# A two-block network on one core: the recurrences' instructions handed to the scheduler 400 places further to the front

## Chip, cores and metric

The kernel runs on one core of a Trainium2 chip. The metric is device time in microseconds (us) of one execution. The engines are called as the profile calls them: PE (TensorE, matrix multiplication), PEld (its weight loads), DVE (VectorE), ACT (ScalarE), POOL (GpSimd), SP (SyncE, which issues the DMAs).

## What is computed

The reference is two transformer-like blocks of width 1024 on 256 tokens, in float32. The first block has two attentions, a cross-attention to 256 memory tokens and a gated feed-forward net with a convolution. The second block has two layers over the 256 tokens and 256 context tokens. Each layer mixes by neighbourhood attention, by a convolution and by a recurrence in both directions (RWKV-7, four heads of 64); then comes a dense feed-forward net (layer 0) or one of eight experts with two chosen for each token (layer 1). The recurrence is what the change is about:

```python
def _rwkv7_scan(r, w, k, v, z, b):       # (T, G, H, dh): 512 steps, 2 directions, 4 heads, 64
    def step(S, inp):
        r_t, w_t, k_t, v_t, z_t, b_t = inp
        s_z = jnp.einsum('ghvk,ghk->ghv', S, z_t)
        S = S * w_t[:, :, None, :] + s_z[..., None] * b_t[:, :, None, :] + v_t[..., None] * k_t[:, :, None, :]
        return S, jnp.einsum('ghvk,ghk->ghv', S, r_t)
    _, y = lax.scan(step, jnp.zeros((G, H, dh, dh), jnp.float32), (r, w, k, v, z, b))
    return y
```

The context is scanned first and its last state is the first state of the tokens' scan, so there are four scans of 256 steps in a row: layer 0 context, layer 0 tokens, layer 1 context (only its state is wanted), layer 1 tokens.

## The kernel before

**Streams.** The work is written as Python generators that emit instructions and yield how much they emitted. `par` lets several generators emit in turn, by weights. So the order of emission mixes, for example, a feed-forward net and a recurrence. Behind that, the scheduler of the kernel language makes each engine's list from what was emitted: it takes instructions by their place in the emission as far as what they need allows, and each engine then works through its list strictly in that order. No order is written by hand.

**Stages.** `program` opens and closes buffer pools by stage. Four stages hold a recurrence:

- C0 (426 to about 770 us): `first_ffn` of the first block, the recurrence over the context of layer 0 and its output projection, behind them the context's dense net.
- C1 (about 1003 to 1254 us): that dense net, the recurrence over the tokens of layer 0, behind them the tokens' dense net.
- C2 (1316 to about 1566 us): the rest of the tokens' dense net and the recurrence over the context of layer 1.
- C3 (1566 to about 1854 us): the projections, neighbourhood attention and convolution of layer 1 and the recurrence over the tokens (`mixers`).

Before C0 stands the first block's attention, between C0 and C1 and between C1 and C2 projections and layer 0's attention, and from 1854 us on the experts.

**Full matmuls.** Projections and nets split each fp32 weight slab into a high part `whi` (ACT, L306) and the rest `wlo` (DVE, L307) and add three fp32r matmuls for each product (`mm3`). They write the PSUM tiles `acc` and `accA`, use the whole array (128*128 in the rows below), and have 256 columns.

**Partial matmuls.** The recurrence is cut into four chunks of 64 steps for each pair of heads; `rwkv_unit` makes one unit for each direction (`dr`) and pair (`i`), and PSUM tile `c0` belongs to direction 0, `c1` to direction 1 (the rows below say `c` for both). A unit inverts a triangular 64x64 matrix by doubling, five rounds that depend on each other, each round one batch of matmuls, a DVE or ACT copy out of PSUM, another batch, another copy:

```python
four = [(a, r, h) for a in range(2) for r, h in ((0, 0), (1, 1), (0, 1), (1, 0))]
...
for a, r, h in four:
    self.mm(pp[half[h], r, P + a * 64:P + a * 64 + 64], X[half[r], h, a, :], i64[half[r]])
if j < 6:
    T1 = tl()
    nc.vector.tensor_tensor(out=T1, in0=two(pp, 0), in1=lm2(j), op=ALU.mult)
Y = tl()
self.copy(Y, two(pp, P))
...
for a, r, h in four:
    self.mm(pp[half[r], h, a * 64:a * 64 + 64], Y[half[h], r, a, :], T1[half[h], r, a, :])
```

These matmuls are fp32 and use a quarter of the array (64*64); `four` lets neighbours use quarters with different rows and columns. Other parts of the recurrence use halves (128*64, 64*128). `rwkv_scan` carries the state from chunk to chunk (`Sb`, `go`) with such matmuls into PSUM tile `sm`. A fp32 matmul leaves two records in the trace: eight matmuls are a row with x16.

Of the kernel before, what the change touches and what calls it, by code (L numbers as in the profile page):

```python
# [148 lines left out]
def par(*gens, behind=None):  # L149


    live = []
    for i, g in enumerate(list(gens) + ([behind] if behind else [])):
        g, w, t = (g + (0.0,))[:3]
        live.append([t / w, i, g, w, None, 0.0])
    spent = 0.0
    while any(e[1] < len(gens) for e in live):
        ready = [e for e in live if (e[4] is None or e[4]()) and e[5] <= spent]
        if not ready:
            late = [e for e in live if e[4] is None or e[4]()]  # L160
            if late:
                t = min(e[5] for e in late)
                yield Lat(t - spent)
                spent = t
            else:
                waits = [e[4] for e in live]
                yield lambda: any(w() for w in waits)
            continue
        e = min(ready, key=lambda e: (e[0], e[1]))
        e[4] = None  # L170
        try:
            c = next(e[2])
        except StopIteration:
            live.remove(e)
            continue
        if callable(c):
            e[4] = c
            continue
        cost = c.cost if isinstance(c, Lat) else c or 1.0
        e[0] += cost / e[3]  # L180
        spent += cost
        if isinstance(c, Lat):
            e[5] = spent + c
        if cost:
            yield cost
# [52 lines left out]
class K:  # L238
# [735 lines left out]
                self.mm(ps[:, c:c + 2], sq[:, i, t * P:(t + 1) * P], self.const("hm"))  # L974
        return ps

    def rwkv(self, l, s, u, S0, need_out, st):

        nc = self.nc
        k_, v_ = u[1], u[2]
        st.update(S={}, units=([], []), begun=[0, 0], done=[0, 0], kd={}, y={})

        sq = self.t("d2", [P, 2, T])
        for i in range(2):
            nc.scalar.activation(sq[:, i, :], k_[:, i, :], AF.Square, scale=self.v(f"k_k{l}", i))
        ps = self.head_sums(sq, "c0")
        nv = self.t("sc", [P, 16])[:, :8]
        nc.vector.tensor_scalar(out=nv, in0=ps[:, 0:8], scalar1=1.0, scalar2=1e-12, op0=ALU.mult, op1=ALU.add)  # L990
        kb = self.head_bc(self.rsqrt(nv, 8), "c0")
        kk = self.t("kk", [P, 2, T])
        for i in range(2):
            nc.vector.scalar_tensor_tensor(out=kk[:, i, :], in0=k_[:, i, :], scalar=self.v(f"k_k{l}", i),
                                           in1=kb[:, i, :], op0=ALU.mult, op1=ALU.mult)

        vt = self.t("vt", [P, 2, T])
        pv = self.ps("c1")
        for t in range(2):
            for i in range(2):  # L1000
                nc.tensor.transpose(pv[:, (2 * t + i) * P:(2 * t + i + 1) * P], v_[:, i, t * P:(t + 1) * P],
                                    self.ident)
        self.copy(vt.rearrange("p a b -> p (a b)"), pv)
        yield 2.0
        yield from par(*[(self.rwkv_maps(l, dr, u, kk, vt, need_out, st), 45) for dr in range(2)],
                       *[(self.rwkv_scan(l, s, dr, u, S0, need_out, st), 12) for dr in range(2)])
        if need_out:
            y = st["y"]
            nc.vector.tensor_tensor(out=y[0], in0=y[0], in1=y[1], op=ALU.add)
            st["o"] = y[0]  # L1010
# [367 lines left out]
    def mixers(self, l, x, kv, u, ao, hp, cv, rwkv):  # L1378

        q, k, v = self.t("qkv", [P, 4, T]), self.t("qkv", [P, 4, T]), self.t("qkv", [P, 2, 512])  # L1380
        pr = self.project(l, 0, x, q, k, v, u, hp, "accA", early=True)
        yield from self.until(pr, "ready")

        def rest():
            yield from self.until(pr, "conv")
            yield from par((na(), 100), (self.conformer(l, hp, cv), 20))

        def na():
            yield from pr
            yield from self.na_attn(l, q, k, v, *kv, ao, "accA", "opM")  # L1390
        yield from par((rest(), 130), (rwkv, 93.5))
# [457 lines left out]
```

## Time and profile before

| | |
|---|---|
| median of 3 runs | 2905.23 us (2900.95 to 2911.19) |
| the profiled execution | 2904.22 us, its span 2902.0 us |
| PE busy | 2721.5 us, 94% of the span |
| DVE busy | 2130.2 us, 73% |
| ACT busy | 1703.9 us, 59% |
| DMA | 619.81 MB, 214 GB/s on average |

The span is what the trace covers; the execution takes 2.2 us more. Busy time is the time in which an engine works on at least one instruction. The rows of the trace give start, duration and form of each instruction. Two starts of PE that follow each other say more than a duration, since matmuls are pipelined and overlap.

### The profile page before, as it was taken

The numbers are of one execution on the slowest core, as the hardware profiler recorded it, in microseconds if no ns is written. First come the engines' busy times: TensorE is split into PE (matmuls) and PEld (weight loads), VectorE is DVE, ScalarE is ACT, GpSimd is POOL, SyncE is SP. The second block draws the span as 40 slices with busy tenths as digits, with TensorE's granted clock in tenths as the row PEclk, the third lists the DMA queues.
The fourth block names the chain that finished last, engine by engine and source line by source line (L and its number), as shares of the span: only waits on it lengthen the run. The fifth ranks groups of instructions, "written<-read, shape, count | busy, mean of one in ns | idle before, by whom it ended". The sixth has DMA issues, their size and how long they took to land.

```text
span 2902.0 us, 55553 instructions
## 1 busy us (share of the span) xinstructions
PE 2721.5 (94%) x22026; PEld 2340.4 (81%) x22026; DVE 2130.2 (73%) x3912; ACT 1703.9 (59%) x2709; POOL 79.8 (3%) x229
## 2 busy tenths in 40 slices
PE   7899989999799899999998878799999999999998
PEld 5788888999787688999997866688888878887886
DVE  4458657777668466777566864689888889989897
ACT  4455555554454355455444553478777777777775
POOL 0000000100000000000000010000000000000000
PEclk9899998999899999999999987799999999999998
DMA  7666432345466723444443221479899999999994
GB/s 269 230 196 196 154 101 89 125 125 153 147 215 223 236 85 100 146 147 152 140 139 107 92 59 29 201 282 364 342 347 359 350 350 354 358 338 356 365 353 168
DMA packets 144022, 619.81 MB, mean 214 GB/s; under 512 B 31044, under 2 KB 38536, under 8 KB 100744
## 3 DMA queue, kind: packets, MB, share of 16 engines
q1 hardware_dynamic: 143752, 616.17, 61.0%
q8 instruction: 175, 2.87, 0.4%
q14 instruction: 95, 0.78, 0.1%
HBM read 615.04 MB, written 1.07 MB: 212 GB/s over the span
## 4 chain that ended last, share of the span: by engine, by line
PE 75%; DVE 8%; ACT 4%; issue 2%; DMA 2%; POOL 0%; SPq 0%; ACTq 0%; POOLq 0%; DVEq 0%
PE acc L291 42%; PE py L291 10%; PE accA L291 8%; PE sm L291 6%; PE c L291 6%; DVE wlo L307 1%; DVE wlo L440 1%; PE md L291 1%; PE sm L1571 1%; ACT whi L306 1%; PE accA L505 0%; DMA raw<-mod_w 0%; ACT whi L439 0%; DVE x L939 0%; DVE t L380 0%
## 5 line engine op out<-in xcount | busy, mean ns | idle before, releaser
L440 DVE TENSOR_TENSOR wlo<-raw,whi 128x1024 fp32r<-128x1024 f32 x666 | 779.4, 1220 | 79.8 <-ACT whi L439 73.0
L306 ACT ACTIVATE whi<-raw 128x512 fp32r<-128x512 f32 x764 | 474.3, 629 | 502.1 <-PE acc L291 259.7
L307 DVE TENSOR_TENSOR wlo<-raw,whi 128x512 fp32r<-128x512 f32 x764 | 521.3, 689 | 330.2 <-ACT whi L306 316.8
L439 ACT ACTIVATE whi<-raw 128x1024 fp32r<-128x1024 f32 x666 | 676.7, 1058 | 105.6 <-PE py L291 60.8
L291 PE MATMUL acc<-whi,op 128*128 128x512 f32 (+1 forms) x2048 | 620.8, 379 | 0.0
L291 PE MATMUL acc<-op,whi 128*128 128x256 f32 x2880 | 561.4, 294 | 8.7 <-ACT op L385 3.6
L291 PEld LDWEIGHTS acc<-op,whi 128*128 128x128 f32 x2880 | 460.1, 196 | 36.3 <-issue 13.8
L291 PEld LDWEIGHTS acc<-whi,op 128*128 128x128 f32 x2048 | 378.6, 189 | 71.5 <-issue 3.0
L291 PE MATMUL acc<-op,wlo 128*128 128x256 f32 x1440 | 414.7, 288 | 10.3 <-DVE wlo L307 10.3
L291 PE MATMUL acc<-wlo,op 128*128 128x512 f32 (+1 forms) x1024 | 393.0, 384 | 2.5 <-DVE wlo L440 1.4
L291 PEld LDWEIGHTS acc<-op,wlo 128*128 128x128 f32 x1440 | 281.5, 196 | 13.1 <-DVE wlo L307 12.7
L291 PE MATMUL py<-whi,ht 128*128 128x512 f32 x896 | 291.2, 396 | 0.5 <-ACT ht L306 0.5
L291 PE MATMUL accA<-opM,whi 128*128 128x256 f32 x1408 | 272.0, 292 | 7.7 <-ACT opM L306 3.5
L291 PEld LDWEIGHTS accA<-opM,whi 128*128 128x128 f32 x1408 | 225.0, 196 | 23.7 <-issue 7.7
L291 PEld LDWEIGHTS acc<-wlo,op 128*128 128x128 f32 x1024 | 193.2, 189 | 53.6 <-DVE wlo L440 17.6
L291 PE MATMUL acc<-fh,whi 128*128 128x256 f32 x1056 | 206.1, 293 | 3.0 <-ACT fh L306 1.9
L291 PE MATMUL accA<-opM,wlo 128*128 128x256 f32 x704 | 202.4, 288 | 1.5 <-DVE wlo L307 1.3
L291 PEld LDWEIGHTS py<-whi,ht 128*128 128x128 f32 x896 | 168.7, 188 | 39.3 <-ACT ht L306 0.9
L291 PE MATMUL py<-wlo,ht 128*128 128x512 f32 x448 | 180.6, 403 | 0.3
L291 PEld LDWEIGHTS acc<-fh,whi 128*128 128x128 f32 x1056 | 165.4, 192 | 18.4 <-issue 9.6
L291 PE MATMUL acc<-fh,wlo 128*128 128x256 f32 x528 | 150.4, 285 | 1.9 <-DVE wlo L307 1.9
L291 PEld LDWEIGHTS accA<-opM,wlo 128*128 128x128 f32 x704 | 137.3, 195 | 4.5 <-issue 2.2
(338 smaller groups left out, 3337.2 us busy)
## 6 DMA issues: line engine op xcount, KB each, us to landing
raw<-moe_up SPq DMA_DIRECT2D x112, 1024.0 KB, 7.0
raw<-moe_gate SPq DMA_DIRECT2D x111, 1024.0 KB, 6.8
raw<-moe_down SPq DMA_DIRECT2D x110, 1024.0 KB, 6.8
raw<-w_in SPq DMA_DIRECT2D x120, 512.0 KB, 3.7
raw<-mod_w SPq DMA_DIRECT2D x96, 512.0 KB, 4.5
raw<-ffn_gate SPq DMA_DIRECT2D x44, 512.0 KB, 3.6
raw<-ffn_up SPq DMA_DIRECT2D x44, 512.0 KB, 3.6
raw<-ffn_down SPq DMA_DIRECT2D x40, 512.0 KB, 3.7
```

The lines of the kernel that those rows point to most:

```text
L291: return self.nc.tensor.matmul(out, lhsT, rhs, start=start, stop=stop, **k)
L306: self.nc.scalar.activation(hi, src, AF.Copy)
L307: self.nc.vector.tensor_tensor(out=lo, in0=src, in1=hi.bitcast(F32), op=ALU.subtract)
L439: self.nc.scalar.activation(hi, raw[:, k:k + g, :], AF.Copy)
L440: eng.tensor_tensor(out=lo, in0=raw[:, k:k + g, :], in1=hi.bitcast(F32), op=ALU.subtract)
L1571: nc.tensor.transpose(pt[:, c * P:(c + 1) * P], h[:, c * P:(c + 1) * P], self.ident)
```

## The change

`rwkv` becomes a wrapper. Its former body is now called `recurrence`, and each of its steps is emitted inside `tc.high_priority(400)`: the scheduler treats every instruction of the four recurrences as if it had been emitted 400 places earlier. What is emitted, its order of emission, the buffers and the arithmetic stay; the output projections behind two of the recurrences (`mix_out`) aren't inside.

```diff
-    def rwkv(self, l, s, u, S0, need_out, st):
+    def rwkv(self, *a):
+
+        gen = self.recurrence(*a)
+        while True:
+            with self.tc.high_priority(400):
+                try:
+                    c = next(gen)
+                except StopIteration:
+                    return
+            yield c
+
+    def recurrence(self, l, s, u, S0, need_out, st):
```

What the scheduler makes of it shows in the engines' lists. Names end in the tile's number; `acc`, `whi`, `wlo`, `op` and `fh` belong to a net, `c`, `zt`, `cst`, `t`, `go`, `Sb` and `vt` to a recurrence; the last figure is the size written.

The first place is on PE in C2, one round of one unit. Before:

```order
L291 MATMUL acc_17395<-op_15121,whi_17373 128x256
L291 MATMUL acc_17395<-op_15120,wlo_17374 128x256
L291 MATMUL c_3058_17408<-t_3045_17332,zt_16553 64x64 x8
L291 MATMUL c_3058_17408<-cst_72,t_3045_17332 64x64 x8
L291 MATMUL c_3061_17429<-t_3047_17351,t_3048_17353 64x64 x8
L291 MATMUL acc_17395<-op_15120,whi_17391 128x256
L291 MATMUL acc_17395<-op_15121,whi_17391 128x256
```

The same round with the change:

```order
L291 MATMUL c_3058_17408<-t_3045_17332,zt_16553 64x64
L291 MATMUL c_3061_17429<-t_3047_17351,t_3048_17353 64x64
L291 MATMUL c_3058_17408<-cst_72,t_3045_17332 64x64
L291 MATMUL acc_16595<-op_15120,whi_16626 128x256
L291 MATMUL c_3058_17408<-cst_72,t_3045_17332 64x64
L291 MATMUL acc_16595<-op_15121,whi_16626 128x256
L291 MATMUL c_3058_17408<-cst_72,t_3045_17332 64x64
L291 MATMUL acc_16595<-op_15120,wlo_16627 128x256
L291 MATMUL c_3058_17408<-cst_72,t_3045_17332 64x64
L291 MATMUL acc_16595<-op_15120,whi_16626 128x256
```

The batch of eight into `c_3058_17408` stood in one piece behind `acc_17395`; now it stands beside the earlier `acc_16595`, and single matmuls of the two alternate.

The second place is on PE in C0, a step of the scan (`sm_6487`) and the first batch of a unit (`c_1189_6475`). Before:

```order
L291 MATMUL acc_6423<-op_4846,wlo_6420 128x256
L291 MATMUL c_1189_6475<-cst_72,zt_6361 64x64 x8
L291 MATMUL sm_6487<-go_5971,Sb_6176 64x64 x6
L291 MATMUL acc_6423<-op_4846,whi_6457 128x256
L291 MATMUL acc_6423<-op_4847,whi_6457 128x256
```

With the change:

```order
L291 MATMUL sm_6487<-go_5971,Sb_6176 64x64
L291 MATMUL c_1189_6475<-cst_72,zt_6361 64x64
L291 MATMUL acc_5655<-op_4846,wlo_5603 128x256
L291 MATMUL sm_6487<-go_5971,Sb_6176 64x64
L291 MATMUL c_1189_6475<-cst_72,zt_6361 64x64
L291 MATMUL acc_5655<-op_4846,whi_5602 128x256
L291 MATMUL sm_6487<-go_5971,Sb_6176 64x64
L291 MATMUL c_1189_6475<-cst_72,zt_6361 64x64
```

Here too batches have come apart into a rotation of three streams, one full matmul in each turn.

The third place is on PE in C1, both directions' units: `c_2387_13477` is copied to `t_2388_13486` by DVE, which the batch into `c_2395_13526` reads. Before:

```order
L291 MATMUL c_2387_13477<-t_2380_13441,t_2381_13443 64x64 x8
L291 MATMUL c_2389_13488<-t_2383_13454,zt_12975 64x64 x8
L291 MATMUL c_2389_13488<-cst_72,t_2383_13454 64x64 x8
L291 MATMUL acc_13513<-fh_13112,whi_13458 128x256
...
L291 MATMUL acc_13513<-fh_13112,wlo_13459 128x256
L291 MATMUL c_2395_13526<-t_2388_13486,zt_13025 64x64 x8
```

With the change:

```order
L291 MATMUL c_2389_13488<-t_2383_13454,zt_12975 64x64
L291 MATMUL c_2387_13477<-t_2380_13441,t_2381_13443 64x64
L291 MATMUL c_2389_13488<-t_2383_13454,zt_12975 64x64
L291 MATMUL c_2389_13488<-cst_72,t_2383_13454 64x64 x8
L291 MATMUL c_2395_13526<-t_2388_13486,zt_13025 64x64 x8
L291 MATMUL c_2395_13526<-cst_72,t_2388_13486 64x64 x6
```

Twelve full matmuls stood between the batches of this round and the next; now none does, and the two directions' first batches alternate.

## Rows read from the trace of the kernel before

**Rows 1.** The page: PE's busy share, then PE and its clock in 40 slices.

```profile
PE 2721.5 (94%) x22026; PEld 2340.4 (81%) x22026; DVE 2130.2 (73%) x3912; ACT 1703.9 (59%) x2709; POOL 79.8 (3%) x229
...
PE   7899989999799899999998878799999999999998
...
PEclk9899998999899999999999987799999999999998
```

**Rows 2.** Windows: the four stages, then the recurrences' dense stretches in C0 and C2.

```profile
core 0: us, PE busy (x) PEld busy (x) DVE busy (x) ACT busy (x) POOL busy (x), PEclk, DMA share, GB/s
426.00:771.00 345.00, 321.35 (x3610) 298.76 (x3610) 250.46 (x583) 181.71 (x329) 18.62 (x50) 0.94 0.41 126
1003.00:1254.00 251.00, 235.38 (x2987) 218.57 (x2988) 178.30 (x430) 130.74 (x238) 13.71 (x45) 0.96 0.35 112
1316.00:1566.00 250.00, 238.72 (x3045) 224.99 (x3043) 164.41 (x350) 121.74 (x213) 12.88 (x49) 0.99 0.41 130
1566.00:1854.00 288.00, 241.28 (x2768) 204.47 (x2768) 188.07 (x537) 135.63 (x291) 23.24 (x53) 0.86 0.27 79
452.50:677.00 224.50, 220.80 (x2915) 206.61 (x2913) 167.16 (x387) 121.16 (x226) 11.40 (x30) 0.99 0.39 119
1316.00:1545.00 229.00, 226.41 (x2813) 214.72 (x2815) 153.93 (x311) 114.55 (x197) 11.60 (x43) 1.00 0.43 139
```

**Rows 3.** Longest wait of PE in C0, 452.5 to 677 us: total, times, longest.

```profile
PE acc L291 <- ACT whi L306: 1.8, 3, 0.7
```

**Rows 4.** Timeline of PE in C0: batches and full matmuls. Start, duration, what.

```profile
486.72 0.41 PE L291 MATMUL c<-t,zt 64*64 64x64 f32 x16
486.96 0.41 PE L291 MATMUL c<-cst,t 64*64 64x64 f32 x16
487.30 0.50 PE L291 MATMUL acc<-fh,whi 128*128 128x256 f32 x2
487.64 0.28 PE L291 MATMUL acc<-fh,wlo 128*128 128x256 f32 x1
487.76 0.40 PE L291 MATMUL acc<-fh,whi 128*128 128x256 f32 x2
...
488.71 0.28 PE L291 MATMUL acc<-fh,wlo 128*128 128x256 f32 x1
488.92 0.29 PE L291 MATMUL c<-t,t 64*64 64x64 f32 x4
```

**Rows 5.** Timeline of PE in C2 where single full matmuls stand between quarters.

```profile
1534.08 0.34 PE L291 MATMUL c<-t,t 64*64 64x64 f32 x6
1534.35 0.38 PE L291 MATMUL acc<-fh,whi 128*128 128x256 f32 x1
1534.66 0.34 PE L291 MATMUL c<-t,t 64*64 64x64 f32 x6
1534.93 0.39 PE L291 MATMUL acc<-fh,whi 128*128 128x256 f32 x1
```

**Rows 6.** Waits of PE in C3, 1600 to 1808 us.

```profile
PE c L291 <- ACT t L301: 4.7, 6, 2.4
PE c L291 <- DVE t L1260: 3.4, 5, 1.3
```

**Rows 7.** Windows: a part of C3, the end of C2, C3's second half.

```profile
1740.00:1770.00 30.00, 25.86 (x482) 17.72 (x476) 12.91 (x45) 10.91 (x32) 2.18 (x2) 0.72 0.10 19
1520.00:1564.00 44.00, 33.96 (x645) 30.69 (x646) 25.45 (x70) 16.87 (x33) 1.29 (x6) 0.96 0.25 76
1690.00:1808.00 118.00, 94.24 (x1135) 68.29 (x1132) 61.08 (x222) 51.17 (x135) 18.71 (x34) 0.77 0.14 25
```

**Rows 8.** Timeline of PE in the first of these windows.

```profile
1760.26 0.65 PE L291 MATMUL c<-t,zt 64*64 64x64 f32 x16
1760.69 0.65 PE L291 MATMUL c<-cst,t 64*64 64x64 f32 x16
```

## The prediction

> **What bounds the kernel now.** I began with the page: PE is busy 94% of the span and in most slices 90% or more at the full clock, DVE 73%, ACT 59% [rows 1]. As a busy share is an average, I cut the span at the stages with a recurrence [rows 2]. In C0 PE is busy 321.35 of 345 us, in C1 235.38 of 251, in C2 238.72 of 250, in C3 241.28 of 288; DVE comes second everywhere. Inside the dense stretches, where recurrence and net run together, almost nothing is left: 220.80 of 224.50 us in C0, 226.41 of 229.00 in C2, the clock at 0.99 and 1.00. The view of waits says the same of C0: PE's largest group of waits is 1.8 us in three times [rows 3]. So in C0 and C2 PE works through its list without a stop, and the recurrence's dependent chain, which has many short steps, is hidden behind full matmuls. An order that finishes this chain sooner has nothing to win there. Whatever it makes PE's own list cost, in starts from one matmul to the next, is paid in full, since PE has 2.6 to 3.7 us of slack in each of these stretches.
>
> Idle time of PE that another order could remove lies at the end of C2 (44.00 less 33.96, 10.0 us) and in the second half of C3 (118.00 less 94.24, 23.8 us) [rows 7].
>
> **What a matmul costs in its neighbourhood.** The timeline gives starts. A batch of eight quarter matmuls in a row takes 0.24 us (486.72 to 486.96), a full matmul among its like 0.12 us (487.64 to 487.76) [rows 4]. Going from one kind to the other costs extra. The last batch before a full matmul takes 0.34 us instead of 0.24 (486.96 to 487.30). The first two full matmuls take 0.34 instead of 0.24 (487.30 to 487.64). From the last full matmul to the next quarter it is 0.21 instead of 0.12 (488.71 to 488.92) [rows 4]. That is 0.10 + 0.10 + 0.09 = 0.29 us for leaving the full matmuls' form and coming back, a round trip, apart from a slower start of the quarters, which these rows don't separate.
>
> Single full matmuls between quarters occur a few times before. Their turn, one full matmul and three or four quarters, takes 0.58 us (1534.08 to 1534.66 and 1534.35 to 1534.93) [rows 5]. The work in it is 0.12 for the full one and at most 0.12 for four quarters, half a batch. The remaining 0.34 us is the price of a round trip, with the start of the quarters in it.
>
> The Trainium skill, TensorEngine Tiling (Array Packing), section Tiling Modes, has a rule that speaks against this change: changing the tiling mode, and not merely the tile, drains TensorE. It names no price; the rows above agree with it. By that rule changes between partial forms count too; they grow by about 40, which at half a round trip (0.17) would make the sum 7 us larger.
>
> **The change, part by part.** Nothing is added or removed on any engine; DMAs keep their order but for a few places, and the buffers are the same. What changes is the order of the lists, and I counted on PE's list, stage by stage, how many stretches of full matmuls it has. Every stretch is one round trip.
>
> - C0: 55 stretches before, 244 after, of which 197 hold one full matmul (1 before). The number of matmuls is the same, 1333 full and 761 partial ones. The second place shown in the section on the change is typical.
> - C1: 43 before, 43 after.
> - C2: 46 before, 348 after, 296 with one full matmul (2 before). The first place is typical.
> - C3: 51 before, 63 after.
>
> The extra round trips are 189 + 0 + 302 + 12 = 503. At 0.34 us: C0 64.3, C2 102.7, C3 4.1, together **171 us**. I take 0.34 and not 0.29 since the turns in rows 5 are the ones that the new list is made of. No row shows a turn with a single quarter matmul, and 180 (C0) and 244 (C2) of the new partial stretches hold just one. Below, the price is 0.19: entering (0.09) and the slow first full matmul (0.10) with nothing for leaving. Above, it is 0.68, twice 0.34, if PE is at half its clock (rival 1). Over 503 trips these are 96 and 342 us. No cover hides any of it: PE is the engine that is waited for, and ACT and DVE only get more time.
>
> The second part is new waits. In C1 (third place) twelve full matmuls, 1.44 us, stood between the batches of a round and the batch that reads DVE's copy of them; now one batch of eight does, 0.24 us. I took for each copy the work on PE between the last matmul that it reads and the first that reads it, by the durations above. Under 0.6 us it is in 8 places of C1 (0 before), 4 of C0 (0), 0 of C2 (5) and 11 of C3 (9); between 0.6 and 1.2 us in 15 (2), 12 (0), 6 (1) and 14 (11). What such a place costs C3 shows already: 11 waits of `c` for L301 and L1260 took 8.1 us, 0.74 each [rows 6]. I price the first kind at 0.7 us and the second at 0.3. C0: 2.8 + 3.6 = 6.4. C1: 5.6 + 3.9 = 9.5. C2: -3.5 + 1.5 = -2.0. C3: 1.4 + 0.9 = 2.3. Together **16 us**, with bounds of 0 (the scheduler's guess of readiness holds) and 32 (each twice as long, behind a slab's split on DVE).
>
> The third part is the tail of C2. Before, no full matmul stands behind the recurrence's last `c` matmul in that stage; after, 243 do. The recurrence then no longer drags behind, and up to 10.0 us of idle time [rows 7] could go. But C3 begins with the norm of the net's result, and its chain of small steps, which the recurrence covered in part, would then stand alone. I count 0, with bounds of -10 and +5.
>
> Against the profiled execution (2904.22 us, 1 us under the median of the runs, 2905.23): 2904.2 + 171 + 16 + 0 = 3091; I say **3090 us**, 6.4% longer.
>
> **Rivals.**
>
> 1. *The clock falls where the forms alternate.* Between 1740 and 1770 us PE is busy 25.86 of 30 us with small matmuls, and the granted clock is 0.72 [rows 7]; a batch of eight there takes 0.43 us instead of 0.24 [rows 8], the lower of the two levels. There PE also waits between its batches, and the few turns of rows 5 were run at the full clock. If a third of the 503 round trips fell to 1.2 GHz, each would cost 0.34 us more, 57 us, and the work in them some 0.24 us more each, 40 us: 3090 + 97 = 3187 us.
>
> 2. *A single change of form is cheap.* One quarter matmul between full ones might cost less than the two ends of a longer stretch. For it speaks that no row shows a turn with one quarter; against it, that the turns with three or four cost as much as the long stretches' two ends together. At 0.10 us the 503 trips cost 50, and the time is 2904 + 50 + 16 = 2970 us.
>
> 3. *The other sign: the recurrences leave the end of their stages.* If the idle 10.0 us at the end of C2 and 23.8 us in C3 [rows 7] vanish because the chain starts earlier, 33.8 us are won. This decides only when a round trip costs less than (33.8 - 16) / 503 = 0.035 us, a tenth of what rows 4 and 5 show; with trips free it gives 2904 - 34 + 16 = 2886 us. Against it also speaks that C3's list changes least: 36 full matmuls stood behind the last `c` matmul there, and 35 do now.
>
> 4. *The change does little.* In C1 and C3 the number of round trips hardly moves. Were C0 and C2 like that, the waits alone would be left, 16 us less 10 at the tail: 2910 us. The lists shown exclude it for the order, so it needs free round trips too.
>
> **How the numbers follow.** The forecast has 0.75, rival 1 0.12, rival 2 0.07, rival 3 0.03, rival 4 0.03. The range of the forecast itself goes from 2904 + 96 + 16 - 10 = 3006 us (price 0.19) to 3091 plus the second 16 us of waits, 5 at C2's tail and half of rival 1's 97, 3160 us. I give 3010 to 3170, which leaves out most of rival 1 and rivals 2 to 4. About 0.3% (9 us) is what a measurement of this kernel can tell from no change. Faster than that is rival 3, 0.03; within it falls rival 4, 0.03; slower is everything else, 0.94.
>
> **What would show it.** In the profile after, C0's dense stretch should be about 65 to 70 us longer with PE still busy over 95% of it, C2's about 100 us, C1 some 10 us with new waits of `c` for L1260 and L301 (by their lines after the change, 11 further down), C3 within 10 us, and the experts from the same start to end as before. The number and the durations of the matmuls should be the same, only their starts further apart: a turn of one full and one or two quarter matmuls should take 0.4 to 0.6 us. PE's granted clock in C0 and C2 tells rival 1 from the forecast; a turn under 0.3 us shows rival 2. The prediction is wrong if the long stretches of C0 and C2 don't grow, or if they grow through PE's waits and not through its starts.

## The result and the profile after

The changed kernel takes 3283.91 us (median of 4 runs, 3276.36 to 3311.96) beside 2908.21 us for the kernel before (4 runs on the same chip, 2900.95 to 2911.5). The ratio is 1.1322, with a 95% interval of 1.1289 to 1.1355: 376 us longer, about twice the 186 us that were forecast. The profiled execution (3311.96 us, span 3310.2 us) is the longest of the four; its span is 408 us longer than that of before.

The page of the changed kernel, PE's busy share, then PE and its granted clock in 40 slices, answers to [rows 1]:

```profile
PE 3128.0 (94%) x22026; PEld 2584.6 (78%) x22026; DVE 2137.4 (65%) x3912; ACT 1703.8 (51%) x2709; POOL 78.3 (2%) x229
...
PE   7999989999989999999999989778999999999998
...
PEclk9999977679989999996795599778999999999998
```

The count of PE's instructions is the same, its busy share is the same, and its busy time is 407 us longer. So nearly everything that was lost lies inside PE's busy time. The clock row has two new hollows, at slices 6 to 9 (C0) and 19 to 23 (C2). The windows of the four stages, each from the same place on PE's list to the same place as in the kernel before, and the experts, answer to [rows 2, 7]. C1, C2 and C3 between these places before (C0 stands in [rows 2]):

```profile
1050.00:1191.80 141.80, 135.47 (x2012) 124.19 (x2011) 96.80 (x243) 70.00 (x133) 9.80 (x26) 0.98 0.32 100
1328.00:1558.00 230.00, 224.41 (x2930) 211.98 (x2929) 151.50 (x308) 113.47 (x199) 11.76 (x44) 1.00 0.41 130
1583.00:1808.00 225.00, 193.80 (x2454) 159.73 (x2452) 149.45 (x432) 109.00 (x243) 23.24 (x53) 0.86 0.24 65
```

All four with the change, and the experts:

```profile
core 0: us, PE busy (x) PEld busy (x) DVE busy (x) ACT busy (x) POOL busy (x), PEclk, DMA share, GB/s
454.50:830.00 375.50, 369.87 (x2914) 296.96 (x2912) 169.35 (x386) 122.67 (x228) 10.11 (x30) 0.79 0.22 71
1200.20:1348.00 147.80, 141.83 (x2011) 127.15 (x2011) 97.29 (x243) 68.40 (x132) 9.83 (x26) 1.00 0.30 96
1483.90:1940.50 456.60, 451.92 (x2934) 348.50 (x2934) 151.02 (x305) 112.81 (x196) 9.36 (x40) 0.72 0.21 66
1968.00:2221.00 253.00, 213.17 (x2456) 170.47 (x2455) 156.15 (x444) 108.03 (x243) 23.02 (x53) 0.84 0.20 57
2396.00:3300.00 904.00, 897.67 (x4064) 724.15 (x4062) 796.21 (x791) 678.58 (x766) 0.00 (x0) 1.00 0.91 340
```

| stretch | before, us | after, us | difference | granted clock, before and after |
|---|---|---|---|---|
| C0, dense part | 224.5 | 375.5 | +151.0 | 0.99, 0.79 |
| C1, dense part | 141.8 | 147.8 | +6.0 | 0.98, 1.00 |
| C2, without its tail | 230.0 | 456.6 | +226.6 | 1.00, 0.72 |
| C3, to the recurrence's end | 225.0 | 253.0 | +28.0 | 0.86, 0.84 |

The experts take about as long as before, 904.0 us beside 902.8. PE's idle time in C0 went from 3.7 us to 5.6 (375.50 less 369.87) and in C2 from 5.6 (230.0 less 224.41) to 4.7: the two long stretches grew in PE's starts and not in its waits. C1 grew within PE's busy time too: its idle time was 6.3 us before and is 6.0.

The timeline of PE in C0 shows how, at two places 4 us apart (start, duration, what):

```profile
590.26 0.33 PE L291 MATMUL c<-bcst,t 128*64 128x64 f32 x2
590.52 0.39 PE L291 MATMUL acc<-op,whi 128*128 128x256 f32 x1
590.83 0.33 PE L291 MATMUL c<-bcst,t 128*64 128x64 f32 x2
...
594.28 0.58 PE L291 MATMUL acc<-op,whi 128*128 128x256 f32 x1
594.79 0.47 PE L291 MATMUL c<-vt,zt 64*64 64x64 f32 x2
595.20 0.58 PE L291 MATMUL acc<-op,whi 128*128 128x256 f32 x1
```

A turn of one full and one partial matmul (x2, two records) takes 0.57 us at 590.26 and 0.92 us at 594.28. Nothing waits in either. The second is at half the clock: the granted clock has two levels, 2.4 GHz (1.0) and 1.2 GHz (0.5), so a mean of 0.79 over 375.5 us says that some 2 x 0.21 x 375.5 = 158 us of C0 ran at the lower one, and 0.72 that 256 us of C2 did. Before it was 4 us and none.

C3 lost in part by a wait. In the view of waits PE stood for the neighbourhood attention's softmax (the row of `t`, written by ACT at L902) 12.7 us before and 25.8 us after. Before the change, 1583 to 1808 us:

```profile
PE sm L291 <- ACT t L902: 12.7, 7, 5.6
```

With it, 1968 to 2221 us:

```profile
PE sm L291 <- ACT t L902: 25.8, 7, 8.5
```

Other waits shrank, so PE's idle time in C3 grew by 8.6 us in all (31.2 to 39.8) of the stage's 28; the other 19 us lie within its busy time.

### The profile page after: what moved, and what is told of

Same layout as the page of the kernel before. It is cut to its first block, busy times and chain, and to the rows that moved or that the text cites. A ratio compares the mean times of both kernels' runs of the same rounds, so it can differ in the third digit from the quotient of the medians.

```text
span 3310.2 us, 55526 instructions
## 1 busy us (share of the span) xinstructions
PE 3128.0 (94%) x22026; PEld 2584.6 (78%) x22026; DVE 2137.4 (65%) x3912; ACT 1703.8 (51%) x2709; POOL 78.3 (2%) x229
## 4 chain that ended last, share of the span: by engine, by line
PE 48%; DVE 3%; ACT 1%; issue 1%; DMA 0%; SPq 0%; POOL 0%; POOLq 0%; DVEq 0%; ACTq 0%
PE acc L291 27%; PE py L291 9%; PE c L291 6%; PE accA L291 3%; PE sm L291 3%; DVE wlo L440 1%; PE sm L1582 1%; DMA opM<-rpb 0%; ACT whi L439 0%; PE accA L505 0%; DVE x L939 0%; SPq L879 0%; DVE wlo L307 0%; ACT t L901 0%; POOL opM L881 0%
## 5 line engine op out<-in xcount | busy, mean ns | idle before, releaser
L291 PE MATMUL acc<-op,whi 128*128 128x256 f32 x2880 | 657.4, 318 | 7.3 <-ACT op L385 3.6
L291 PEld LDWEIGHTS acc<-op,whi 128*128 128x128 f32 x2880 | 504.1, 209 | 55.5 <-issue 13.4
L291 PE MATMUL acc<-op,wlo 128*128 128x256 f32 x1440 | 455.0, 316 | 10.1 <-DVE wlo L307 10.1
L291 PEld LDWEIGHTS acc<-op,wlo 128*128 128x128 f32 x1440 | 300.6, 209 | 25.4 <-DVE wlo L307 12.5
L291 PE MATMUL acc<-fh,whi 128*128 128x256 f32 x1056 | 258.6, 327 | 6.0 <-ACT fh L306 3.0
L291 PE MATMUL c<-t,t 64*64 64x64 f32 (+6 forms) x2304 | 215.2, 277 | 12.5 <-ACT t L301 7.0
L291 PEld LDWEIGHTS acc<-fh,whi 128*128 128x128 f32 x1056 | 188.2, 209 | 34.2 <-issue 10.8
L291 PEld LDWEIGHTS c<-t,t 64*64 64x64 f32 (+3 forms) x2304 | 153.4, 166 | 66.8 <-issue 28.8
```

What stands on the lines that cost most here:

```text
L291: return self.nc.tensor.matmul(out, lhsT, rhs, start=start, stop=stop, **k)
```

## Experiments

Two theories were set against each other. **A**: the single matmuls that alternate cost the time, by the starts and by the clock. **B**: that the recurrence is ahead costs the time, since the net's full matmuls then lack it as cover, or their slabs come late. The shift moves both things at once; the experiments part them.

### 400 places ahead, batches whole

Every step of a recurrence is still emitted 400 places ahead, but each further matmul of the step gets one place more, so that all of them keep the place of the first and a batch of eight stays in one piece:

```diff
     def mm(self, out, lhsT, rhs, start=True, stop=True, **k):
-        return self.nc.tensor.matmul(out, lhsT, rhs, start=start, stop=stop, **k)
+        if self.glue is None:
+            return self.nc.tensor.matmul(out, lhsT, rhs, start=start, stop=stop, **k)
+        self.glue += 1
+        with self.tc.high_priority(self.glue):
+            return self.nc.tensor.matmul(out, lhsT, rhs, start=start, stop=stop, **k)
...
             with self.tc.high_priority(400):
+                self.glue = 0
...
```

> The recurrences stand 400 places ahead as in the change, but the matmuls of one step keep one place, so that a batch stays whole: PE's list has 295 stretches of full matmuls instead of 805 (302 before the change), and the recurrence's last matmuls of C0 to C3 stand as far ahead as with the change (within 15 full matmuls but for 150 in C1 and 30 in C2). Theory A (the single matmuls that alternate cost the time, by their starts and by the clock): 2895 to 2925 us, C0's dense stretch about 225 us, C2's about 230. Rival B (the recurrence's being ahead costs the time, by what the net's full matmuls then lack as cover or by slabs that come late): about 3280 us, as with the change.

Measured: 2926.06 us, ratio 1.0045 (1.0024 to 1.0065). The windows of C0 and C2 in this run:

```profile
450.80:680.00 229.20, 222.54 (x2915) 208.73 (x2912) 167.72 (x386) 122.36 (x228) 15.01 (x30) 0.98 0.36 117
1330.00:1565.00 235.00, 229.74 (x2934) 214.84 (x2934) 150.00 (x305) 112.63 (x196) 9.85 (x39) 0.99 0.39 128
```

229.2 and 235.0 us instead of 375.5 and 456.6, at a clock of 0.98 and 0.99. Of the 376 us some 362 go away with the alternation, though the recurrence is as far ahead. Theory A holds; the 14 us that stay (1 us above its estimate) go with the recurrence's being ahead, B's share at most. In the profiled execution, 24 us longer than that of before, 14 of them lie in C3 counted up to the experts, and 9 in C2 with its tail.

### 3000 places ahead, and 12

One number changed in each:

```diff
-            with self.tc.high_priority(400):
+            with self.tc.high_priority(3000):
```

> 3000 places instead of 400: the recurrences stand as far ahead as what they need lets them, and PE's list has 311 stretches of full matmuls, near the 302 before the change. Theory A (alternation): 2900 to 2930 us. Rival B (being ahead costs): 3280 us or more, since it is further ahead in C0 and C2 than with 400 places.

> 12 places instead of 400: the recurrence's last matmuls stand where they stood before the change, but the list has 1194 stretches of full matmuls, 892 more than before the change and 389 more than with it. Theory A: at the 0.75 us for each added stretch that the change cost, 2908 + 669 = 3577 us; at 0.45 us (full clock alone) 2908 + 401 = 3309 us. Rival B (being ahead costs): 2900 to 2940 us.

Measured: 2966.57 us for 3000 places (ratio 1.0167, 1.0134 to 1.0200), 3545.84 us for 12 places (one run, between theory A's two sums and near the upper one). Twelve places do more harm than 400, and 3000 do an eighth of it, 49 us by the ratio. The price is not in how far the recurrence moves but in what it is merged with. A step's matmuls carry consecutive places; moved by 12 or by 400, they fall among the places of a chunk of the net's full matmuls, and the list takes them by turns. Moved by 3000, they are in front of everything that is ready, and each batch goes as soon as it can, in one piece. The windows of C0 and C2 with 12 places:

```profile
450.20:879.30 429.10, 426.73 (x2915) 326.52 (x2912) 169.08 (x386) 121.62 (x225) 11.24 (x30) 0.75 0.19 62
1602.00:2111.60 509.60, 503.02 (x2934) 385.13 (x2933) 154.21 (x308) 113.76 (x198) 9.90 (x44) 0.70 0.18 59
```

PE is busy all the time here too, and the clock is lower still. But 2966.57 us is 37 us above theory A's upper end: B has a small share, in the profiled execution 24 us in C0, 17 in C2 with its tail and 20 in C3 up to the experts. The window of C0 with 3000 places shows the form it takes, 248.7 us with PE idle for 10.1 of them (3.7 before):

```profile
452.20:700.90 248.70, 238.56 (x2914) 219.28 (x2912) 169.50 (x386) 121.93 (x228) 10.13 (x30) 0.96 0.33 108
```

### A turn by itself

This kernel issues series of turns and nothing else that would disturb PE. Its core, shortened (`full`: fp32r, 128x128, 256 columns; `quarter`: fp32, 64x64; in `same` a fp32 matmul of the whole array stands in place of `quarter`):

```python
full(f, 0)
for i in range(8):
    quarter(q, i)
for _ in range(times):
    for _ in range(nf):
        full(f, k); k += 1
    for _ in range(nq):
        quarter(q, j); j += 1
```

> Leaves out the whole reference: it copies the input to the output and runs, on PE, series of turns of full fp32r matmuls (128x128, 256 columns) and fp32 quarter matmuls (64x64), each behind 300 full matmuls in a row. In the series called one a turn is one full and one quarter matmul; two and four have two and four quarters; batch has twelve full and eight quarters; same has one full and one fp32 matmul that uses the whole array (64 columns); three has three full and one quarter; quarters has quarters alone. The prediction's price (0.34 us for a round trip, with 0.12 for the full matmul and 0.03 for a quarter) gives turns of 0.49, 0.52, 0.58, 2.02 us for one, two, four and batch and 0.73 for three at the full clock. The theory after the result (0.42 to 0.45 us for a round trip with a single quarter) gives 0.57 to 0.60 for one. If the change of array form makes the price, same has a turn under 0.35 us; if the change of number type makes it, same has about what one has. If alternation itself lowers the clock, the granted clock falls below 0.8 in one, two and four, and stays at 1.0 in batch and in the full matmuls between; if something else of the kernel lowers it (the other engines' work), it stays at 1.0 in all.

The timeline of PE in four of the series:

```profile
59.08 0.39 PE L32 MATMUL one<-h 128*128 128x256 f32 x1
59.39 0.32 PE L39 MATMUL one<-x 64*64 64x64 f32 x2
59.65 0.38 PE L32 MATMUL one<-h 128*128 128x256 f32 x1
...
63.18 0.58 PE L32 MATMUL one<-h 128*128 128x256 f32 x1
63.69 0.47 PE L39 MATMUL one<-x 64*64 64x64 f32 x2
64.09 0.58 PE L32 MATMUL one<-h 128*128 128x256 f32 x1
...
588.59 0.39 PE L32 MATMUL four<-h 128*128 128x256 f32 x1
588.90 0.34 PE L39 MATMUL four<-x 64*64 64x64 f32 x8
589.17 0.38 PE L32 MATMUL four<-h 128*128 128x256 f32 x1
...
859.69 1.69 PE L32 MATMUL batch<-h 128*128 128x256 f32 x12
861.32 0.46 PE L39 MATMUL batch<-x 64*64 64x64 f32 x16
861.71 1.70 PE L32 MATMUL batch<-h 128*128 128x256 f32 x12
...
1020.40 0.37 PE L32 MATMUL same<-h 128*128 128x256 f32 x1
1020.60 0.33 PE L42 MATMUL same<-x 128*128 128x64 f32 x2
1020.74 0.36 PE L32 MATMUL same<-h 128*128 128x256 f32 x1
```

A turn with one quarter takes 0.57 us (59.08 to 59.65), with four 0.58 (588.59 to 589.17): up to four quarters cost next to nothing on top. A turn of twelve full and eight quarters takes 2.02 us (859.69 to 861.71), the forecast's number; its price is 2.02 - 12 x 0.12 - 0.24 = 0.34 us. For a single quarter it is 0.57 - 0.12 - 0.03 = 0.42. In `same`, fp32r and fp32 alternate as well, but both use the whole array, and the turn takes 0.34 us: the form makes the price, not the number type.

The windows of `one`, the start of `two`, `batch`, `same` and `quarters` show the clock:

```profile
63.00:284.00 221.00, 221.00 (x728) 138.39 (x727) 0.00 (x0) 0.00 (x0) 0.00 (x0) 0.50 0.00 0
326.00:339.00 13.00, 13.00 (x115) 8.57 (x115) 0.00 (x0) 0.00 (x0) 0.00 (x0) 1.00 0.01 1
859.00:981.00 122.00, 121.96 (x1697) 109.63 (x1697) 0.00 (x0) 0.00 (x0) 0.00 (x0) 1.00 0.01 2
1019.00:1105.00 86.00, 86.00 (x762) 86.00 (x760) 0.00 (x0) 0.00 (x0) 0.00 (x0) 1.00 0.00 1
1302.60:1356.20 53.60, 31.42 (x1934) 29.50 (x1936) 0.00 (x0) 0.00 (x0) 0.00 (x0) 1.00 0.02 4
```

With one quarter for each full matmul the clock falls after seven turns, at 63 us, and stays at 0.50 for the rest of the series, with DVE, ACT and the DMA at rest and no gap in PE's records. `four` falls after six turns, `two` only after some 23 (it is still at 1.00 from 326 to 339 us), and both stay at 0.50 then. In `batch`, `same` and `three` the clock stays at 1.00, and in `quarters` too, though PE stands idle there for 22 of 53.6 us, between groups of quarters. So such turns lower the clock without any help from the other engines, and idle time in PE's records is neither needed for the fall nor, in groups like these, enough. Whether it is the change of form as such that counts, or that so little is computed in each microsecond of such turns, the series don't part.

### Other forms, and turns in bursts

The same kernel with other series.

> Leaves out the whole reference, like the run with series of turns, with other series. half: one full fp32r matmul and one fp32 matmul of half the array (128x64). onetype: one fp32 matmul of the whole array (64 columns) and one fp32 quarter. mixed: one quarter and one half matmul, no full one. six: six full and one quarter. rare: twenty times four turns of one full and one quarter, then 48 full in a row; often: the same with sixteen turns. If the array form makes the price, half and onetype have a turn above 0.5 us at the full clock (0.9 at half), and mixed two changes of form in each pair, above 0.4 us; if the number type makes it, onetype and mixed stay under 0.35 us. six is 0.42 + 6 x 0.12 + 0.03 = 1.17 us. If alternation lowers the clock only when it lasts, rare stays at 1.0 and often falls in each of its bursts; if the form alone decides, both fall.

The timeline of two of them at the full clock, a fp32 matmul of the whole array beside a fp32 quarter, and a quarter beside a half:

```profile
202.70 0.43 PE L50 MATMUL onetype<-x 128*128 128x64 f32 x2
203.06 0.32 PE L39 MATMUL onetype<-x 64*64 64x64 f32 x2
203.32 0.43 PE L50 MATMUL onetype<-x 128*128 128x64 f32 x2
...
366.68 0.33 PE L39 MATMUL mixed<-x 64*64 64x64 f32 x2
366.93 0.33 PE L43 MATMUL mixed<-x 128*64 128x64 f32 x2
367.19 0.33 PE L39 MATMUL mixed<-x 64*64 64x64 f32 x2
```

`onetype` takes 0.62 us a turn with one number type and two forms. `mixed` takes 0.51 us for a pair. The work in it is 0.03 for the quarter and about 0.06 for the half (eight halves up to a full matmul take 0.61 us, eight quarters 0.39), which leaves about 0.21 us for each change of form: a change between two partial forms costs about as much as one from the whole array, half of 0.42. `half` has 0.57 us like the quarter, and `six` 1.17 us (70.0 us for 60 turns), as forecast. The windows of `six`, of bursts of four turns and of bursts of sixteen, each burst before 48 full matmuls:

```profile
503.00:573.00 70.00, 70.00 (x495) 58.01 (x495) 0.00 (x0) 0.00 (x0) 0.00 (x0) 1.00 0.00 1
611.00:771.00 160.00, 160.00 (x1197) 144.33 (x1198) 0.00 (x0) 0.00 (x0) 0.00 (x0) 1.00 0.00 1
809.00:1202.00 393.00, 392.77 (x1920) 306.79 (x1920) 0.09 (x1) 0.05 (x1) 0.00 (x0) 0.70 0.00 1
```

In the first two the clock stays at 1.00. In the third it is 0.70 in the mean: it falls in each burst and comes back in the full matmuls behind. `half`, `onetype` and `mixed` fall to 0.50 as well, `half` after some 23 turns.

### The change by halves, and 1000 places

```diff
         gen = self.recurrence(*a)
+        if not a[1] == 0:
+            yield from gen
+            return
```

leaves the shift to the two recurrences over the tokens; with `a[1] == 1` it is left to those over the context.

> The 400 places for the two recurrences over the tokens alone (C1 and C3); those over the context (C0, C2) stay as before the change. PE's list has 316 stretches of full matmuls (302 before the change). Theory A with stages that don't act on each other: C1 6 us and C3 with its tail 24 us longer, as in the profile of the change, 2908 + 30 = 2938 us. Rival (the whole loss comes from C0 and C2 and what C3 lost there was only pushed on from them): 2900 to 2915 us.

> The 400 places for the two recurrences over the context alone (C0 and C2); those over the tokens (C1, C3) as before the change. 791 stretches of full matmuls. If the stages' losses add up: the 376 us of the change less the 23 us that the tokens' two cost alone, 2908 + 353 = 3261 us. Rival (the four recurrences need each other's shift to lose): below 3200 us.

Measured: 2930.11 us for the tokens alone (ratio 1.0081, 1.0056 to 1.0106) and 3265.97 us for the context alone (1.1251, 1.1231 to 1.1272). By the ratios these are 23.5 and 363.8 us; their sum, 387 us, stands beside 384 us for the whole change by its own ratio. The stages lose apart from each other. In the run with the tokens' shift alone C3 takes 249.3 us (225.0 before, 253.0 with the whole change), and the view of waits gives half of the reason:

```profile
PE sm L291 <- ACT t L902: 27.3, 7, 8.4
```

PE's idle time there is 42.9 us, 11.7 more than before, of 24.3 that the stage lost; the rest lies within its busy time.

The windows of C0 and C2 with the context's shift alone:

```profile
452.90:823.50 370.60, 364.47 (x2916) 292.70 (x2912) 169.30 (x386) 122.63 (x228) 10.10 (x30) 0.80 0.22 72
1474.90:1910.80 435.90, 431.22 (x2935) 335.34 (x2934) 151.03 (x305) 112.84 (x196) 9.13 (x40) 0.77 0.21 69
```

C2's list alternates here as with the whole change (347 stretches of full matmuls in both traces), and yet it takes 435.9 us and not 456.6. What differs is the clock, 0.77 and not 0.72: 200 us at the lower level instead of 256.

> 1000 places instead of 400: 492 stretches of full matmuls, of the 190 added ones 172 in C2, 12 in C3, 5 in C0, 1 in C1. Theory A (0.75 us for each added stretch, and 25 to 55 us for the recurrences' being ahead, as runs with few stretches had): 2908 + 143 + 25 to 55 = 3076 to 3106 us, with C2's dense stretch 110 to 150 us longer and its granted clock below 0.85, and C0's within 25 us of before. Rival (the loss grows with the number of places): above 3284 us.

Measured: 3085.91 us (one run), inside theory A's range. C2 without its tail:

```profile
1352.50:1714.80 362.30, 355.38 (x2937) 291.00 (x2936) 150.57 (x305) 113.79 (x197) 9.10 (x40) 0.81 0.26 83
```

It took 362.3 us instead of 230.0, 132 more and at a clock of 0.81, as theory A expected. C0, with 5 added stretches, took 252.4 us at 0.98, about what it took with 3000 places; that is 28 us more than before, where at most 25 were expected. The loss doesn't grow with the number of places.

### Two attempts to gain

The first gathers a recurrence's steps at multiples of 200 places, batches whole, to have fewer round trips than before:

```diff
-            with self.tc.high_priority(400):
+            with self.tc.high_priority(1 + self.tc.cur_priority % 200):
+                self.glue = 0
...
```

> A version that uses the finding the other way: no fixed number of places; every step of the recurrences of C0, C1 and C2 is put to the front as far as the last multiple of 200 places, and its batches stay whole; C3 is as before the change. Stretches of full matmuls: 283 instead of 302 (C0 46 instead of 60, C1 40 instead of 45, C2 47 instead of 48). Theory A: 20 round trips fewer at 0.42 us, 2908 - 8 = 2900 us, ratio 0.997. Rival (an order that isn't that of before costs by its waits, as with 3000 places): 2915 to 2930 us.

Measured: 2922.97 us, ratio 1.0055 (1.0036 to 1.0075). The rival was right. C0's dense stretch took 234.5 us instead of 224.5, with PE idle for 11.0 us of them (3.7 before), though it had 14 round trips fewer. Six microseconds of trips were bought with 7 of waits. That leaves 9 us; the clock, 0.98 instead of 0.99, took some of them, and the rest stays open. The profiled execution, 2936.49 us, is the longest of the six.

The second leaves the recurrences alone and puts C3's neighbourhood attention ahead, whose wait had grown:

```diff
+            att = self.na_attn(l, q, k, v, *kv, ao, "accA", "opM")
+            while True:
+                with self.tc.high_priority(60):
...
```

> The recurrences as before the change. In C3 the neighbourhood attention, whose waits for its softmax grew when the recurrence went ahead there (12.7 us before, 25.8 with the change), is put 60 places to the front instead, with its batches whole; PE's stretches of full matmuls grow by 1, its changes between partial forms by 14 (at 0.2 us 3 us). If the wait is a matter of what PE has to do behind the attention's batches: 8 to 12 us less wait and 3 us more starts, 2898 to 2903 us, ratio 0.997 to 0.999. Rival (the softmax on DVE and ACT bounds it, whatever PE does): 2908 to 2915 us.

> As the run with the attention 60 places ahead, with 250 places. If more cover behind the batches is what counts: 2895 to 2902 us. Rival (the attention's own dependent chain then stands bare at the end of the recurrence or takes the recurrence's cover): 2910 to 2930 us.

Measured: 2914.66 us with 60 places (ratio 1.0021, 1.0009 to 1.0033) and 2929.22 us with 250 (1.0086, 1.0073 to 1.0099). With 60 the waits for L902 (L907 in this kernel) fell from 12.7 us to 10.1 in two groups, and others grew; C3 took 6 us longer in all. With 250 places that wait was 9.6 us and C3 took 14 us longer. Both times fit the rivals and not the hopes: more work behind the attention's batches hardly shortens the wait for its softmax. The largest group of that wait with 60 places:

```profile
PE sm L293 <- ACT t L907: 8.6, 3, 4.4
```

None of these versions beats the kernel before; what is shown says undo the change, or keep batches whole if a shift is wanted.

## Why the prediction was off by half

- **Where PE loses.** Right. PE stayed without slack in C0 and C2, its waits there moved by less than 2 us, and the loss came through the starts. The experts didn't change. C1 grew by 6.0 us where 10 were forecast, but that is luck: 9.5 of the forecast were waits, and PE's idle time there didn't grow (6.3 and 6.0 us).
- **The number of round trips.** Right as the quantity: batches kept whole take the loss away, and twelve places with 1194 stretches lose more than 400 with 805.
- **The price of a round trip, 0.34 us.** Here the sum was too small. The step was "The work in it is 0.12 for the full one and at most 0.12 for four quarters ... The remaining 0.34 us is the price". The turn of 0.58 us in [rows 5] was read rightly, but a turn doesn't get shorter when quarters are missing: with one, two and four it takes 0.57 to 0.59. With a single quarter the price is 0.42, and 491 trips in C0 and C2 cost 206 us and not 167. The prediction had said that no row shows such a turn, and its bounds held 0.42; what it chose was the value for a batch.
- **The clock.** This is the larger miss. Rival 1 had a chance of 0.12 and a third of the trips, 97 us, and the sum itself had nothing for the clock, on the ground that the turns of [rows 5] ran at the full clock. But those were a few turns, and the series show that few turns (four in a burst) don't lower it and many do. At the lower level a turn takes 0.92 us instead of 0.57, so of each microsecond there 0.38 are lost. C0: 154 more microseconds, 59 lost. C2: 256, 97 lost. Together 156 us that the sum didn't have, of the 408 of the profiled execution, the longest of four. Rival 1 had each turn at the lower level 0.58 us longer, where 0.35 is measured; what it had far too low was how much of the time runs there.
- **Both together.** C0: 189 x 0.42 + 59 = 138 us of 151 measured. C2: 302 x 0.42 + 97 = 224 of 227. The same two numbers, applied to the run with 12 places, give for C2 375 trips, 158 us, and 2 x 0.30 x 509.6 = 306 us at the lower level, 116 us: 274 of 280 measured (509.6 less 230.0). With 1000 places C2 has 172 trips more, 72 us, and 2 x 0.19 x 362.3 = 138 us at the lower level, 52: 124 of 132. With the context's shift alone C2 has 200 us at the lower level, 76: 203 of 206 (435.9 less 230.0). What is left is 3 to 13 us for each stage; in C0, 22 more changes between partial forms at 0.21 would be 5 of them.
- **The spread of the runs** bears out the 0.38. The longest of the four executions with the change has a span of 3310.2 us at a mean granted clock of 0.900, the shortest 3274.6 us at 0.914. That is 662 and 563 us at the lower level; 99 us at 0.38 are 38, and the spans are 36 us apart. So in the median run the clock's share is smaller than in the profiled one, by the same estimate about 130 of the 376 us.
- **The waits, 16 us.** Their sum missed C3. In C1 the waits of `c` for L1271 and L301 came, but only 3.2 us in ten times of the 9.5, and another wait shrank by as much (4.2 us for L321 before, 1.1 now). In C3 the recurrence's own copies were priced, 2.3 us, but not that the recurrence covers the attention's softmax: that wait grew by 13 us, PE's idle time by 8.6 and the stage by 28. Of the other 19 us the twelve round trips are 5 at 0.42, and 18 us more at the lower level (81 and 63) 7. Most of C3's loss stays without alternation (21 us in the run with whole batches, up to the recurrence's end like the 28, and 24 with the tokens' shift alone), so it goes with the recurrence's being ahead, theory B.
- **The tail of C2 and rival 3.** The tail took 27.5 us instead of 25.0 (1940.5 to 1968 and 1558 to 1583). Nothing was won there, as forecast, and C3 won nothing either.
- **Rivals 2 and 4** are out: a single quarter between full matmuls isn't cheap.
- **The range** ended at 3170 us since it left rival 1 out. The sum's own upper bound, 0.68 us for each trip, gives 2904 + 342 + 16 = 3262 us, and the range should have reached there; the measured 3283.91 lies 22 us beyond even that.

The Trainium skill, TensorEngine Tiling (Array Packing), section Tiling Modes, on which the prediction drew, says that a change of tiling mode drains TensorE. The series agree that a change costs time, also between two partial forms, and give it a size: 0.42 us for a change there and back round a single quarter. That it is a drain, no run here shows.

What stays open is why C0 lost 13 us more than the two terms give (8 without the changes between partial forms), where C1's 6 us within PE's busy time come from, and 7 of C3's 28. Of the 24 us that C0 lost with 3000 places, PE's idle time explains 6, the clock (0.96 instead of 0.99, 15 us more at the lower level) about 6, and 31 more changes between partial forms (37 in the trace, 6 before) about 6; the last 6 are open. Why the granted clock falls in such turns is open as well: the runs show that it does.

## What to carry to other kernels

A priority offset on one of two streams is a merge of two lists of numbers: look at the merged list before the runs, and see whether batches come apart. Where TensorE's matmuls use different parts of the array, keep those of one form together; each lone one between others costs 0.42 us at the full clock, and in a long alternation the granted clock falls to half too. When a price is taken from a few turns, ask what it becomes when nothing but such turns is left, and put the half clock into the range.

## What the runs showed of the hardware

- A granted clock of 0.50 with PE busy without a gap: 221 us of alternating full and quarter matmuls, nothing else running. The Trainium skill, TensorE: Matmul & The Clock Gate, section "A second HAM failure mode: psum-queue depth-cycling", tells of a clock that goes back and forth where PE idles briefly between groups of matmuls. The records of this series show no idle time between them, and in `quarters`, where they show 22 us of it, the clock stayed at 1.00; whether the array idles inside what they call busy, no run here shows.
- The lower level stretches a turn from 0.57 to 0.92 us, and not to twice that: not all of a turn follows the granted clock.
- In the two kernels of turns the series with four turns in a burst, with three or six full matmuls in a turn and with whole batches stayed at 1.00; the series with one, two and four quarters, with a half, with two partial forms, with a full and a partial fp32 matmul, and the bursts of sixteen fell to 0.50. The fall came after six to some 23 turns.
- The clock also moves stretches that a change doesn't touch. In the run with the attention 60 places ahead, the stretch between C0 and C1 took 204.4 us instead of 198.9 and most of C2 170.5 instead of 165.3, with 14 us at the lower level instead of 3, and 18 instead of none, though PE's list there is that of before. A difference of 6 us in one stage of one profile says little.
